# Block sums of four w_out pairs: made in DRAM by accumulating transfers in place of a page and VectorE additions

## The chip, the cores and the metric

The kernel runs on one core of a Trainium2 chip. The metric is device time in microseconds of one launch; before the change its median over three runs is 1105.4 us (1105.19 to 1105.71). The names used are those of the profile: PE is TensorE's matmuls, PEld its weight loads, DVE is VectorE, ACT is ScalarE, POOL is GpSimd, and SP is SyncE, whose in-order queue issues nearly all loads.

## The reference

One encoder block on x (256 tokens by 2048 channels), float32 throughout:

```python
hn = rmsnorm(h, mix_norm_pre)
z, xbc, dt_raw, u = split(hn @ w_in)
y_ssd = ssd_mixer(z, xbc, dt_raw, ...)   # bidirectional Mamba-2 scan, 16 heads
y_pool = pool_mixer(u, pool_w, pool_scale)
mix = concatenate([y_ssd, y_pool]) @ w_out          # w_out 2048 x 2048
h = h + rmsnorm(mix, mix_norm_post)
ff = conv_glu(rmsnorm(h, ffn_norm_pre), ...)         # 2048 -> 2 x 5632 -> 2048
h = h + rmsnorm(ff, ffn_norm_post)
gate = sigmoid(rmsnorm(h, ple_norm_pre) @ w_ple_gate)
h = h + rmsnorm(gate * (p @ w_ple), ple_norm_post)
```

The change lies in how part of `w_out` is made ready for the product `mix`.

## The kernel before

Float32 products are made of three TensorE products each: an operand is split into a high part (rounded to fp32r by an ACT copy, L157) and a low part (a DVE subtraction, L158). Weights arrive from DRAM as 1 MB tiles of 128 partitions by 2048, each a pair of k-blocks for 1024 output columns. `load` (L120) issues each on SP; the tile sits in one of three "raw" buffers, is split into one of five "w" buffers, and is multiplied. A raw buffer is free again when DVE has made the last low part from it, and until then SP waits with the next load, and with everything queued behind it.

The stages in order of time are: dt and pooling input (`dtu`, to about 49 us), the three slabs of `xbc` (`xb2`, `xb0`, `xb1`, 52 to 141 us, four 1 MB loads each), `z` (eight loads, 141 to 196 us) with the last scan products (`yo`, `yd`) between, the output projection (`wo`, 196 to 284 us), the gated feed-forward, its down projection `dn`, and the gate `gt`. Small jobs of the scan and the pooling are put into a list `work`; `aside()` runs one entry of it after every load's products, so that their PE, ACT and DVE instructions lie between those of the slabs. A scheduler sets the final order on each engine from the order of the code and its own model of times; a table of costs is not part of the program.

Some pairs of `w_out`, `w_down` and `w_gate` are multiplied by a scheme with seven block products for eight (`seven_products`), which needs, of the four 512-column blocks v0 to v3 of a weight tile, the sums that `add_blocks` makes (L275): v1+v0, v0+v3, v3+(v1+v0) and v2+v3+v1+v0. For four pairs of `w_out`, named (0, 0), (0, 2), (1, 0) and (1, 2) by output half and k-block, these sums are made early, while `xbc` and `z` run:

- `early_fetch` takes a page (one of 13 shared 1 MB buffers) and loads the pair into it (tile `wob`).
- `early_add` makes the sums in place with four DVE additions of 128 x 512, and GpSimd stores the page to a DRAM tile `wos` (L265).
- At 208.6 to 244.0 us `seven_products` loads `wos` back as `wo00t`, `wo02t`, `wo10t` and `wo12t`, and splits and multiplies it (`wo00c`, `wo00d` and so on).

What the steps below touch besides: `rz` and `yn0m` (the norm of y after the scan, small POOL operations at L804 and L410), `dec` (L608, POOL), `seg`, `E`, `cb`, `cv` (scan and convolution jobs on ACT, DVE and PE), `pw`, `mx`, `cath`, `catl` (pooling) and `sp` (the softplus of dt, a chain of small DVE operations at L577 to L589).

Of the kernel before, what the change touches and what calls it, by code (L numbers as in the profile page):

```python
# [11 lines left out]
F32 = mybir.dt.float32  # L12
F32R = mybir.dt.float32r
AF = mybir.ActivationFunctionType
ALU = mybir.AluOpType
ORDERED = (mybir.EngineType.Activation, mybir.EngineType.DVE, mybir.EngineType.SP)

P = 128
# [35 lines left out]
def build(nc, a, out):  # L54
    x = a["x"][0]

    w_dtu, w_xbc, w_z, w_out, w_up = a["w_dtu"], a["w_xbc"], a["w_z"], a["w_out_"], a["w_up"]
# [3 lines left out]
    with tile.TileContext(nc) as tc, \  # L61
# [9 lines left out]
        def ins(r):  # L71
            return getattr(r, "ins", r)

        def page(name, dtype=F32):
            return gp.tile([P, 2048], dtype, tag="pg", bufs=13, name=name)

        def mid(name, dtype=F32):
            return gp.tile([P, 1024], dtype, tag="mid", bufs=3, name=name)
# [4 lines left out]
        def main(name):  # L83
            return [pm.tile([P, 512], F32, tag="main", name=f"{name}_{i}") for i in range(2)]
# [30 lines left out]
        last, sums_ = {}, {}  # L115

        def load(dst, src, ahead=False):

            with tc.issue_after(last["dma"]) if last and not ahead else nullcontext():
                return ins(nc.sync.dma_start(dst, src))  # L120
# [79 lines left out]
        work = []  # L200
# [31 lines left out]
        def block_sums(name, w, c0, k, held):  # L232


            pg = []

            def fetch():
                r = page(f"{name}b{c0}_{k}")
                pg.append(r)
                load(r, w[c0 // 1024, k // 2])  # L240

            def add():
                add_blocks(pg[0])
                if held:
                    sums_[name, c0, k] = pg[0], True

            def store():
                if not held:
                    t = dp.tile([P, 2048], F32, tag=f"{name}s{c0}_{k}", bufs=1, name=f"{name}s{c0}_{k}")
                    nc.gpsimd.dma_start(t, pg[0])  # L250
                    sums_[name, c0, k] = t, False

            return fetch, add, store

        early_raw = {}

        def early_fetch(c, k):
            early_raw[c, k] = page(f"wob{c}_{k}")
            load(early_raw[c, k], w_out[c, k // 2])

        def early_add(c, k):
            r = early_raw.pop((c, k))
            add_blocks(r)
            t = dp.tile([P, 2048], F32, tag=f"wos{c}_{k}", bufs=1, name=f"wos{c}_{k}")
            nc.gpsimd.dma_start(t, r)  # L265
            sums_["wo", c * 1024, k] = t, False

        APART = ("dn",)

        def add_blocks(r, t=None):  # L270

            v = r.rearrange("p (b c) -> p b c", b=4)
            s = v if t is None else t.rearrange("p (b c) -> p b c", b=4)
            for i, a, b in ((1, v, 0), (0, v, 3), (3, s, 1), (2, s, 3)):
                nc.vector.tensor_add(s[:, i], v[:, i], a[:, b])  # L275
# [95 lines left out]
        def feature_major(name, w, get, acc):  # L371

            for u in range(4):
                r = raw(f"{name}r{u}", w[u])
                for j in range(2):
                    wh, wl = split(f"{name}{u}_{j}", r[:, j * 1024:(j + 1) * 1024], 1024)
                    for kk in range(2):
                        k = 4 * u + 2 * j + kk
                        xh, xl = get(k)
                        for f in range(4):  # L380
                            s = slice(kk * 512 + f * P, kk * 512 + (f + 1) * P)
                            for q, (ww, xx) in enumerate(((wh, xh), (wh, xl), (wl, xh))):
                                mm(acc[f // 2][:, f % 2 * L:(f % 2 + 1) * L], ww[:, s], xx,
                                   k == 0 and q == 0 and f % 2 == 0, k == NK - 1 and q == 2)
                aside()
# [19 lines left out]
        def rms(name, parts, scale, n=1):  # L405

            base = EPS
            for i, q in enumerate(parts):
                m = tiny(f"{name}m{i}", n)
                nc.gpsimd.tensor_scalar(m, q, scale, base, op0=ALU.mult, op1=ALU.add)  # L410
                base = m
            r = tiny(f"{name}r", n)
            nc.gpsimd.tensor_tensor(r, m, mhalf[:, :n], op=ALU.pow)
            return r
# [36 lines left out]
        def times_rows(name, acc, rb):  # L451
            o = mid(name)
            for i in range(2):
                nc.vector.tensor_tensor(o[:, i * 512:(i + 1) * 512].rearrange("p (f t) -> p f t", f=2),
                                        acc[i].rearrange("p (f t) -> p f t", f=2),
                                        rb.unsqueeze(1).to_broadcast([P, 2, L]), op=ALU.mult)
            return o

        def conv(name, acc, taps, wcol, wstep, bcol):

            cv = mid(name)
            half = taps // 2
            for f in range(4):
                o, i = cv[:, f * L:(f + 1) * L], acc[:, f * L:(f + 1) * L]
                nc.scalar.activation(o, i, AF.Identity, bias=vec(bcol + f), scale=vec(wcol + half * wstep + f))
                for j in range(taps):
                    d = j - half
                    if d == 0:
                        continue
                    lo, hi = max(0, -d), L - max(0, d)  # L470
                    nc.vector.scalar_tensor_tensor(o[:, lo:hi], i[:, lo + d:hi + d], vec(wcol + j * wstep + f),
                                                   o[:, lo:hi], op0=ALU.mult, op1=ALU.add)
            return cv
# [15 lines left out]
        for u in range(0, NK, 2):  # L489
            r = [wp.tile([P, 2048], F32, tag="raw", bufs=3, name=f"dtur{u}") if u else r0, page(f"dtur{u + 1}")]  # L490
            for j in range(2):
                k = u + j
# [17 lines left out]
            for j in range(2):  # L510
                k = u + j
# [184 lines left out]
        def xbc(slab):  # L696
            acc = main(f"xbc{slab}")
            feature_major(f"xb{slab}", w_xbc[slab], hn, acc)
            sc = times_rows(f"xr{slab}", acc, rxb)
            cv = conv(f"cv{slab}", sc, 5, V_SCW + 4 * slab, 12, V_SCB + 4 * slab)  # L700
            th = mid(f"th{slab}")
            nc.scalar.activation(th, cv, AF.Tanh, scale=0.5)

            nc.vector.scalar_tensor_tensor(cv, th, 1.0, cv, op0=ALU.add, op1=ALU.mult)
            return cv
# [42 lines left out]
        def job(f, *args):  # L748
            return lambda: f(*args)
# [5 lines left out]
            [job(pool_mix, 2), job(pool_mix, 3), job(decays), job(seg_sums)],  # L755
            [],
        ])
        work[0].append(job(early_fetch, 0, 0))
        work[2].append(job(early_add, 0, 0))
        work[1].append(job(early_fetch, 0, 2))  # L760
        work[3].append(job(early_add, 0, 2))
        work[3].append(job(early_fetch, 1, 0))
        bc = xbc(2)
        work.extend([
            [job(seg, 0), job(seg, 1), job(pool_map, 0), job(pool_map, 1)],
# [1 line left out]
            [job(seg, 4), job(weigh, 0, 0), job(pool_map, 2)],  # L767
            [job(seg, 5), job(pool_map, 3)],
        ])
        work[0].append(job(early_add, 1, 0))  # L770
        xa = xbc(0)
        work.extend([
            [job(seg, 6)],
# [1 line left out]
            [job(xs_turn, xa, 0)],  # L775
            [],
        ])
        xb = xbc(1)
        y = page("y")

# [8 lines left out]
            [job(mix, 0, 1), job(mix, 1, 0)],  # L789
            [job(mix, 1, 1)],  # L790
        ])
        work[4].append(job(early_fetch, 1, 2))
        work[6].append(job(early_add, 1, 2))
        zacc = [main(f"z{t}") for t in range(2)]
        token_major("z", w_z, 0, list(range(NK)), hn, zacc)
        assert not work
# [5 lines left out]
        for t in range(2):  # L802
# [13 lines left out]
            r = rms(f"yn{t}", [ss], rz[t][:, 1:2], n=2)  # L816
# [157 lines left out]
        for i, w_ in enumerate(which[2:] + which[:2]):  # L974
            fetch, add, store = block_sums(*w_, i >= len(which) - 2)
            n = 45 * i // 10 + 4
# [110 lines left out]
        with in_order():  # L1087
            for _ in range(5):
                next_part()
            for n in range(NPIECES):  # L1090
                s, v, i = blocks[n // 4]
# [135 lines left out]
        for half in range(2):  # L1227
# [16 lines left out]
            for t in range(2):  # L1244
                for n, (o, c0) in enumerate(columns(acc[t])):
                    c1 = c0 + o.shape[-1]
                    c = slice(half * 1024 + c0, half * 1024 + c1)

                    th = mid(f"gth{half}{t}{n}")
                    v = th[:, :c1 - c0]  # L1250
# [103 lines left out]
```

## Time and profile before

| | us |
|---|---|
| median of three runs | 1105.4 |
| the profiled execution, its time | 1104.97 |
| its span, first to last instruction | 1103.2 |
| PE busy | 1096.7 (99%) |
| DVE busy | 977.2 (89%) |
| ACT busy | 729.1 (66%) |
| POOL busy | 84.9 (8%) |

The profiled execution took 1104.97 us, 1.8 us more than its span and 0.4 us less than the median. Busy times are sums over the span. Matmuls overlap each other in the pipeline, so that the busy share of PE does not show short delays between matmuls; their starts do. The granted TensorE clock was 0.999 of full speed over the span.

### The profile page before, as it was taken

The page shows a single profiled execution, that of the slowest core. Times are in us where ns is not written, and L with a number is a line of the kernel's source. Part 1 is how long each engine was busy: PE and PEld are TensorE (multiplying, and loading weights), DVE is VectorE, ACT ScalarE, POOL GpSimd, SP SyncE. Part 2 cuts the span into 40 slices and gives each one's busy share as a digit, 9 for nine tenths or more (in the row PEclk, how much of TensorE's full clock was granted, in tenths as well). Part 3 has the DMA queues.
Part 4 walks back from the last instruction along what each step waited for, and adds up shares of the span by engine and source line. Part 5 has one row for each costly group of instructions (what it writes and reads, how often), then busy time and mean ns, then how long its engine had stood idle before and what let it go on. Part 6 is the DMA issues. An engine that isn't in the chain of part 4 may idle for free.

```text
span 1103.2 us, 16052 instructions
## 1 busy us (share of the span) xinstructions
PE 1096.7 (99%) x5961; PEld 948.8 (86%) x5961; DVE 977.2 (89%) x1373; ACT 729.1 (66%) x1068; POOL 84.9 (8%) x145
## 2 busy tenths in 40 slices
PE   9999999999999999999999999999999999999998
PEld 9999988888888888888888888888888888888886
DVE  6589998898868998889889988898999999999997
ACT  6858763566776565655656646657688878786773
POOL 0200000100100000000000000000000000051001
PEclk9999999999999999999999999999999999999999
DMA  9895259556489999989999998999999989996872
GB/s 363 359 339 195 101 183 367 209 195 244 158 367 388 408 397 364 403 344 367 383 366 383 364 391 345 404 362 420 367 410 375 378 335 389 419 379 224 317 276 77
DMA packets 57247, 361.71 MB, mean 328 GB/s; under 512 B 6352, under 2 KB 7504, under 8 KB 21200
## 3 DMA queue, kind: packets, MB, share of 16 engines
q1 hardware_dynamic: 45648, 298.71, 69.0%
q0 software_dynamic: 11088, 61.35, 14.5%
q8 instruction: 47, 0.77, 0.3%
q10 hardware_dynamic: 432, 0.62, 0.2%
q14 instruction: 32, 0.26, 0.1%
HBM read 306.65 MB, written 54.00 MB: 327 GB/s over the span
## 4 chain that ended last, share of the span: by engine, by line
PE 97%; ACT 1%; DVE 1%; issue 0%; POOL 0%; POOLq 0%; DVEq 0%
PE ga L90 22%; PE va L90 22%; PE dna L90 11%; PE woa L90 7%; PE xbc L90 5%; PE gt L90 5%; PE dns L90 4%; PE dtu L90 4%; PE z L90 4%; PE dn0s L90 2%; PE dn1s L90 2%; PE ple L90 1%; PE gts L90 1%; PE wos L90 1%; PE yd L90 1%; PE pw L90 1%
## 5 line engine op out<-in xcount | busy, mean ns | idle before, releaser
L90 PE MATMUL ga<-wox,ug_0w 128*128 128x512 f32 x704 | 130.8, 337 | 0.0
L90 PE MATMUL ga<-wox,ug_1w 128*128 128x512 f32 x704 | 130.2, 337 | 0.0
L90 PE MATMUL va<-wox,uv_0w 128*128 128x512 f32 x704 | 129.2, 337 | 0.0
L90 PE MATMUL va<-wox,uv_1w 128*128 128x512 f32 x704 | 129.2, 337 | 0.0
L90 PEld LDWEIGHTS ga<-wox,ug_0w 128*128 128x128 f32 x704 | 107.7, 188 | 14.6 <-ACT pl L919 0.2
L90 PEld LDWEIGHTS ga<-wox,ug_1w 128*128 128x128 f32 x704 | 107.5, 188 | 14.5 <-DVE wox L195 0.2
L90 PEld LDWEIGHTS va<-wox,uv_1w 128*128 128x128 f32 x704 | 107.5, 188 | 14.5
L90 PEld LDWEIGHTS va<-wox,uv_0w 128*128 128x128 f32 x704 | 107.5, 188 | 14.5
L275 DVE TENSOR_TENSOR dnb<-dnb 128x512 f32<-128x512 f32 x128 | 88.3, 690 | 3.0
L250 POOL DMA_DIRECT2D dns<-dnb x30 | 16.1, 536 | 319.4 <-DVE dnb L275 279.1
L90 PE MATMUL xbc<-hnh,xb_0w 128*128 128x256 f32 x192 | 37.9, 284 | 0.3 <-ACT u L571 0.3
L90 PE MATMUL xbc<-hnh,xb_1w 128*128 128x256 f32 x192 | 37.1, 283 | 0.0
L846 ACT CAST he<-he 128x512 fp32r<-128x512 f32 x13 | 8.1, 621 | 42.6 <-DVE he L845 42.6
L988 ACT CAST hs<-hid 128x384 fp32r<-128x384 f32 (+1 forms) x44 | 23.4, 537 | 13.7 <-PE dna L90 13.5
L90 PEld LDWEIGHTS xbc<-hnh,xb_0w 128*128 128x128 f32 x192 | 30.8, 189 | 0.9 <-ACT u L571 0.4
L90 PEld LDWEIGHTS xbc<-hnh,xb_1w 128*128 128x128 f32 x192 | 30.7, 189 | 0.1
L1068 ACT ACTIVATE fc<-gr,vt 128x256 f32<-128x256 f32 x44 | 26.1, 593 | 6.9 <-DVE gr L1061 6.9
L90 PE MATMUL dna<-dn_0w,hs 128*128 128x512 f32 x108 | 28.6, 394 | 0.0
L90 PE MATMUL dna<-dn_1w,hs 128*128 128x512 f32 x108 | 28.3, 392 | 0.0
L1139 POOL DMA_DIRECT2D hd<-hsum x24 | 12.9, 539 | 193.1 <-PE dn0s L90 70.4
L989 DVE TENSOR_TENSOR hs<-hid,hs 128x384 fp32r<-128x384 f32 (+1 forms) x44 | 25.4, 581 | 2.6 <-ACT hs L988 2.6
L90 PE MATMUL xbc<-hnl,xb_1w 128*128 128x256 f32 x96 | 27.3, 284 | 0.0
(1781 smaller groups left out, 2871.4 us busy)
## 6 DMA issues: line engine op xcount, KB each, us to landing
dnb<-w_down SPq DMA_DIRECT2D x32, 1024.0 KB, 10.0
dns<-dnb POOLq DMA_DIRECT2D x30, 1024.0 KB, 6.5
hd<-hsum POOLq DMA_DIRECT2D x24, 512.0 KB, 8.2
zr<-w_z SPq DMA_DIRECT2D x8, 1024.0 KB, 5.0
dtur<-w_dtu SPq DMA_DIRECT2D x14, 528.0 KB, 8.5
hsum<-he POOLq DMA_DIRECT2D x13, 512.0 KB, 7.7
wo0r<-w_out_ SPq DMA_DIRECT2D x6, 1024.0 KB, 6.2
gtb<-w_gate SPq DMA_DIRECT2D x6, 1024.0 KB, 9.6
```

What stands on the lines that cost most here:

```text
L90: last["pe"] = ins(nc.tensor.matmul(o, lhsT, rhs, start=start, stop=stop, skip_group_check=True))
L250: nc.gpsimd.dma_start(t, pg[0])
L275: nc.vector.tensor_add(s[:, i], v[:, i], a[:, b])
L846: nc.scalar.copy(o[:, :512], s[:, :512])
L988: nc.scalar.copy(t[:, :c1], hid_part(k)[:, :c1])
L989: nc.vector.tensor_sub(t[:, 512:512 + c1], hid_part(k)[:, :c1], t[:, :c1].bitcast(F32))
L1068: nc.scalar.activation(c[:, f], v[:, f], AF.Identity, bias=vec(V_FCB + 4 * s + 2 * i + f), scale=vec(w + NF))
L1139: nc.gpsimd.dma_start(o.bitcast(F32), kept[k])
```

## The change

`early_fetch` and `early_add` go, and with them four pages, the sixteen DVE additions (L275, `wob`) and four stores from GpSimd. In their place stands `sums_in_dram`, with three jobs for each pair:

- `copy`: SP copies the 1 MB of `w_out` to the DRAM tile `wos`, DRAM to DRAM, with no on-chip buffer.
- `pairs_`: two accumulating transfers issued by GpSimd. One adds block 3 of `w_out` to blocks 0 and 2 of `wos`, the other block 0 to blocks 1 and 3. Each has 256 rows of 2 KB.
- `rest`: two more, of 128 rows of 2 KB. One adds block 1 of `wos` to its block 2, the other block 1 of `w_out` to block 3.

The results are the same four sums. The loads back (`wo00t` and the rest), the splits and the products stay. The jobs stand one load apart in `work`, and the last pair's copy moves from the fifth entry of the `z` list to its second.

```diff
-        early_raw = {}
-
-        def early_fetch(c, k):
-            early_raw[c, k] = page(f"wob{c}_{k}")
-            load(early_raw[c, k], w_out[c, k // 2])
-
-        def early_add(c, k):
-            r = early_raw.pop((c, k))
-            add_blocks(r)
+        def sums_in_dram(c, k):
+
             t = dp.tile([P, 2048], F32, tag=f"wos{c}_{k}", bufs=1, name=f"wos{c}_{k}")
-            nc.gpsimd.dma_start(t, r)
-            sums_["wo", c * 1024, k] = t, False
+            src = w_out[c, k // 2]
+            o, v = (u.rearrange("p (b c) -> p b c", b=4) for u in (t, src))
+
+            def add(dst, from_):
+                nc.gpsimd.dma_start(dst, from_, accum_op=ALU.add)
+
+            def copy():
+                load(t, src)
+
+            def pairs_():
+                add(o[:, 0::2], v[:, 3:4].to_broadcast([P, 2, 512]))
+                add(o[:, 1::2], v[:, 0:1].to_broadcast([P, 2, 512]))
+
+            def rest():
+                add(o[:, 2], o[:, 1])
+                add(o[:, 3], v[:, 1])
+                sums_["wo", c * 1024, k] = t, False
+
+            return copy, pairs_, rest
...
-        work[0].append(job(early_fetch, 0, 0))
-        work[2].append(job(early_add, 0, 0))
-        work[1].append(job(early_fetch, 0, 2))
-        work[3].append(job(early_add, 0, 2))
-        work[3].append(job(early_fetch, 1, 0))
+        for n, j in enumerate(sums_in_dram(0, 0)):
+            work[1 + n].append(j)
...
-        work[0].append(job(early_add, 1, 0))
+        for n, j in enumerate(sums_in_dram(0, 2)):
+            work[1 + n].append(j)
...
+        for n, j in enumerate(sums_in_dram(1, 0)):
+            work[1 + n].append(j)
...
-        work[4].append(job(early_fetch, 1, 2))
-        work[6].append(job(early_add, 1, 2))
+        for n, j in enumerate(sums_in_dram(1, 2)):
+            work[1 + n].append(j)
```

On SP, before the change, where the loads of `xbc` (`xb2r`, `xb0r`, `xb1r`) are issued; `wob` is a page of the old way:

```order
L120 DMA poolw<-pool_w_ 128x2048
L120 DMA xb2r_765<-w_xbc 128x2048
L120 DMA wob_0_691<-w_out_ 128x2048
L120 DMA xb2r_866<-w_xbc 128x2048
L120 DMA xb0r_959<-w_xbc 128x2048
L120 DMA xb0r_1075<-w_xbc 128x2048
L120 DMA xb0r_1163<-w_xbc 128x2048
L120 DMA wob_2_763<-w_out_ 128x2048
L120 DMA xb0r_1264<-w_xbc 128x2048
L120 DMA wob_0_928<-w_out_ 128x2048
```

The same place after it:

```order
L120 DMA poolw<-pool_w_ 128x2048
L120 DMA wos_0_633<-w_out_ 16x16384
L120 DMA xb2r_763<-w_xbc 128x2048
L120 DMA xb2r_860<-w_xbc 128x2048
L120 DMA xb0r_948<-w_xbc 128x2048
L120 DMA xb0r_1058<-w_xbc 128x2048
L120 DMA wos_2_945<-w_out_ 16x16384
L120 DMA xb0r_1147<-w_xbc 128x2048
L120 DMA xb0r_1250<-w_xbc 128x2048
```

The first copy stands one place ahead of the first page load, before the third `xb2r` load, and the second copy one place ahead of the second. The third and fourth stand further on, behind the second `xb1r` load and behind the second load of `z`; the fourth page load stood behind all eight loads of `z`.

On POOL, before, from the norm constants `rz` to the norm of y:

```order
L805 TENSOR_SCALAR rz_2055<-rx0r 128x1
L265 DMA wos_0_864<-wob_0_691 128x2048
L608 TENSOR_TENSOR dec<-dec,dt 128x16 x2
L265 DMA wos_2_926<-wob_2_763 128x2048
L265 DMA wos_0_1073<-wob_0_928 128x2048
L265 DMA wos_2_2005<-wob_2_1890 128x2048
L410 TENSOR_SCALAR yn0m_2069<-ss_2060,rz_2055 128x2
```

The same after, as far as the second pair, and the fourth (the third reads as the others do), with the semaphores that each waits for (DMAHW: a transfer of SP, DMASW: one of POOL):

```order
L262 DMA wos_0_633<-w_out_ 256x1x512 [waits DMAHW2_49]
L262 DMA wos_0_633<-w_out_ 256x1x512
L262 DMA wos_0_633<-wos_0_633 128x512 [waits DMASW1_49,DMASW0_49]
L262 DMA wos_0_633<-w_out_ 128x512
L262 DMA wos_2_945<-w_out_ 256x1x512 [waits DMAHW7_49]
L262 DMA wos_2_945<-w_out_ 256x1x512
L618 TENSOR_TENSOR dec<-dec,dt 128x16 [waits DVE_49,Activation_49]
...
L262 DMA wos_2_1666<-w_out_ 256x1x512 [waits DMAHW1_49]
L262 DMA wos_2_1666<-w_out_ 256x1x512
L262 DMA wos_2_1666<-wos_2_1666 128x512 [waits DMASW6_49,DMASW5_49,DMASW4_49]
L262 DMA wos_2_1666<-w_out_ 128x512 [waits DMASW7_49]
L420 TENSOR_SCALAR yn0m_2061<-ss_2052,rz_2047 128x2 [waits Activation_49,Pool_49]
```

Four transfers stand where one stood, POOL waits for the copy before the first and for the first two before the third, and `dec` and `yn0m` stand behind such waits.

On DVE, before, from the end of the second `xb2r` load's split, with the softplus `sp` and the first pair's additions:

```order
L583 TENSOR_TENSOR sp_600<-sp_599 128x64
L275 TENSOR_TENSOR wob_0_691<-wob_0_691 128x512
L584 TENSOR_SCALAR sp_601<-sp_600 128x64
L275 TENSOR_TENSOR wob_0_691<-wob_0_691 128x512
L586 SCALAR_TENSOR_TENSOR sp_601<-sp_601,sp_600 128x64
L275 TENSOR_TENSOR wob_0_691<-wob_0_691 128x512
L586 SCALAR_TENSOR_TENSOR sp_601<-sp_601,sp_600 128x64
L275 TENSOR_TENSOR wob_0_691<-wob_0_691 128x512
L586 SCALAR_TENSOR_TENSOR sp_601<-sp_601,sp_600 128x64
L158 TENSOR_TENSOR xb_0w<-xb2r_866,xb_0w 128x1024
```

The same place after:

```order
L593 TENSOR_TENSOR sp_600<-sp_599 128x64
L594 TENSOR_SCALAR sp_601<-sp_600 128x64
L596 SCALAR_TENSOR_TENSOR sp_601<-sp_601,sp_600 128x64 x6
L597 SCALAR_TENSOR_TENSOR sp_601<-sp_601,sp_599 128x64
L158 TENSOR_TENSOR xb_0w<-xb2r_763,xb_0w 128x1024
L598 TENSOR_SCALAR sp_601<-sp_601 128x64
L158 TENSOR_TENSOR xb_1w<-xb2r_763,xb_1w 128x1024
```

The additions are gone and the softplus now runs ahead of the third load's split, which it stood behind.

## The prediction

> **What bounds the kernel now.** I read the busy times first, then the chain of work that ended last, then the chain piece by piece in the stages that the change touches, then the stretches of time with their DMA share, and last the waits of SP and the rows of single loads.
>
> ```profile
> span 1103.2 us, 16052 instructions
> PE 1096.7 (99%) x5961; PEld 948.8 (86%) x5961; DVE 977.2 (89%) x1373; ACT 729.1 (66%) x1068; POOL 84.9 (8%) x145
> PE 97%; ACT 1%; DVE 1%; issue 0%; POOL 0%; POOLq 0%; DVEq 0%
> ```
>
> TensorE is busy for 99% of the span and is 97% of the chain. Work taken off another engine is worth only what PE loses while it waits for that engine, in the stages where the work lay: `xbc` and `z`, 52 to 196 us. Busy time hides short delays between matmuls, so I count PE's work there by the chain's own pieces, which give a price for each kind:
>
> ```profile
> 52.24 11.71 PE xbc L90 x96
> 71.52 1.85 PE mx L90 x16
> 74.55 1.02 PE dps L90 x8
> 76.02 1.02 PE cps L90 x8
> 90.91 0.23 PE seg L90
> 101.73 0.86 PE cb L90 x4
> 118.38 1.43 PE pw L90 x12
> 134.07 0.88 PE xt L693 x8
> 134.95 5.72 PE xbc L90 x48
> 140.67 22.09 PE z L90 x96
> 182.87 0.86 PE yo L90 x2
> 183.73 1.73 PE yd L90 x16
> 196.31 11.10 PE woa L90 x48
> ```
>
> From the first `xbc` matmul (52.24) to the first of `z` (140.67) pass 88.43 us. By the code that stretch holds 12 loads of 48 `xbc` matmuls (12 x 5.72 = 68.6 us), two groups of 16 `mx` (3.7), `dps` and `cps` (2.0), 48 `pw` (4 x 1.43 = 5.7), two groups of four `cb` (1.7), 16 `seg` (16 x 0.23 = 3.7) and one group of `xt` (0.9): 86.3 us. PE lost at most 2.1 us there, 0.19% of the kernel, and not all of that to waits. From 140.67 to 196.31, 55.64 us, lie two times 96 `z` matmuls (44.2), four groups of `yd` (6.9), four of `yo` (3.4) and one of `xt` (0.9), 55.4 us: it lost 0.2. So no relief of DVE, SP or the pages in these stages can bring more than 2.1 + 0.2 = 2.3 us.
>
> **The change, part by part.** *The additions.* DVE loses the sixteen additions:
>
> ```profile
> L275 DVE TENSOR_TENSOR wob<-wob x16: 678/684/694, 60.3 to 177.4; 128x512 f32<-128x512 f32 x16
> 52.20:140.70 88.50, 88.26 (x705) 85.98 (x706) 82.62 (x153) 61.47 (x104) 3.15 (x5) 1.00 0.57 208
> 78.59 1.05 ACT xb_1w L157
> 88.68 0.48 ACT E L636
> ```
>
> That is 16 x 0.684 = 10.9 us of DVE work, 8.2 us of it in the `xbc` stage, where DVE works 82.6 of 88.5 us (the third of the busy times in the row, after PE and PEld). Yet PE already works there without a break worth 2.1 us, and where the chain does leave PE, from 78.59 to 89.16 us, it runs through ACT, which loses no instruction. So the cover that hides the additions is PE itself; it stays. I take 0.3 us of gain out of the possible 0 to 2.3, nearer to the low end because the row of the chain names ACT and not DVE.
>
> *The new order.* On DVE the softplus comes earlier, and on PE, ACT and DVE the `seg`, `pw`, `cb` and `catl` jobs between 88 and 130 us stand a few rows from where they stood. Nothing in the trace prices a new order. Below, the gain is already in the 2.3 us. Above, I bound it by one split of half a load that comes late as a whole, since a weight tile is the largest thing that PE takes at a time:
>
> ```profile
> 53.70 1.22 DVE L158 TENSOR_TENSOR xb_1w<-xb2r,xb_1w 128x1024 fp32r<-128x1024 f32 x1
> 60.88 1.05 ACT L157 CAST xb_0w<-xb2r 128x1024 fp32r<-128x1024 f32 x1 [3.49 <-DMA xb2r<-w_xbc]
> 73.37 1.19 PE xbc L90 x10
> ```
>
> 1.05 + 1.22 = 2.3 us. I take nothing: the splits run far ahead of PE. The half load that ACT waited 3.49 us for and split at 60.88 is the fourth of its slab, and PE starts on it at 73.37: 12.5 us of lead.
>
> *SP.* Four loads leave the queue and four copies enter it, so its issue time stays. The copies need no page, so SP no longer stands still for one. What it does stand still for is the raw buffers:
>
> ```profile
> SPq L120 <- DVE xb_1w L158: 65.0, 9, 16.3
> 37.64 0.39 SPq L120 DMA_DIRECT2D xb2r<-w_xbc  x1
> 116.72 46.50 SPq L120 DMA_DIRECT2D zr<-w_z  x8
> 40.00:50.00 10.00, 10.00 (x64) 10.00 (x63) 0.36 (x2) 9.86 (x14) 1.44 (x5) 1.00 1.01 420
> 90.00:100.00 10.00, 9.98 (x82) 9.73 (x81) 10.00 (x16) 6.45 (x11) 0.00 (x0) 1.00 0.14 43
> 110.00:120.00 10.00, 10.00 (x80) 9.63 (x79) 9.59 (x16) 8.81 (x15) 0.00 (x0) 1.00 0.21 76
> ```
>
> The first copy is issued where the third `xb2r` load was, at about 38 us, when the DMA engines are full (share 1.01, 420 GB/s, the last two numbers of the row), ahead of the third `xb2r` load. It delays that load by its own 1 MB, 1.05 MB / 420 GB/s = 2.5 us, or twice that if a copy inside DRAM costs a read and a write. PE gets to that load at 52.24 + 2 x 5.72 + 1.85 = 65.5 us, over 25 us after its issue, so this is hidden. The second copy passes two `xb0r` loads, the third two `xb1r` loads, the fourth six `z` loads, each by the same 2.5 to 5 us against a lead of 12.5: nothing.
>
> *The accumulating transfers.* For each pair they write 2 x 256 + 2 x 128 = 768 rows of 2 KB, 1.57 MB, where one 1.05 MB store was; the page load becomes the copy. No row shows an accumulating transfer. The nearest are these:
>
> ```profile
> poolw<-pool_w_ SPq DMA_DIRECT2D x1, 1024.0 KB, 11.7
> wos<-wob POOLq DMA_DIRECT2D x4, 1024.0 KB, 4.7
> out<-vg SPq DMA_DIRECT2D x6, 256.0 KB, 2.8
> ```
>
> At the 26 GB/s per engine of the full stretch, a 2 KB row takes 0.08 us and the 48 rows that each of 16 engines gets take 3.7 us a pair; below that it cannot go. The high end is a row that waits out a whole transfer, 2.8 us by the shortest landing shown: 48 x 2.8 = 134 us a pair. I take the low end doubled for the two operands, 7.5 us a pair, because the nearest row, the store by the same queue to the same tile, landed in 4.7 us, only 2.2 us over its bytes. One sentence of the Trainium skill bears on this, in "Collectives: The Full Stack", section "The bandwidth ceiling": a reducing transfer runs at half the rate of a copy because it has two sources to read, while the addition is free. No run so far shows it; by it the estimate would be 7.5 us a pair, by the plain row 3.7, and neither comes near the points below.
>
> With 2.2 us of landing a step, a pair then takes 12 us or so for its copy (11.7 at worst, as `poolw` in the full stretch), and 7.2 and 4.7 us for its two steps. The first pair is ready at about 38 + 12 + 12 = 62 us, the last, whose copy goes out behind the second `z` load (the eight spread over 46.50 us from 116.72) at about 123 us, at about 147. What waits for them is late:
>
> ```profile
> 63.47 0.77 POOL L265 DMA_DIRECT2D wos<-wob  x1 [21.32 <-DVE sp L586]
> 194.98 0.58 POOL L410 TENSOR_SCALAR yn0m<-ss,rz 128x2 f32<-128x2 f32 x1 [16.09 <-ACT zt L815]
> 208.64 0.37 SPq L120 DMA_DIRECT2D wo00t<-wos  x1
> 216.85 1.05 ACT L157 CAST wo00dw<-wo00t 128x1024 fp32r<-128x1024 f32 x1 [1.03 <-DMA wo00t<-wos]
> ```
>
> Behind POOL's new waits stand `dec`, used by the `yo` products (182.87 us in a row above), and `yn0m` at 194.98; on SP `wo00t` waits from 208.64. All have some 50 us or more. POOL's own cost, 16 issues for 4 at the 0.77 us of the first row, perhaps double for 256 rows, is some 18 us of an engine that is 8% busy.
>
> **Sum.** Additions -0.3, new order 0, SP 0, transfers 0: the profiled execution's 1104.97 us would become 1104.7. The median stands 0.4 us above that execution, so I predict 1105.4 - 0.3 = 1105.1 us.
>
> **Rivals.** *Slow accumulation crowds out the weights (slower).* A load has 64 KB for each engine, eight packets of 8 KB, 0.31 us each at 26 GB/s. If the engines take turns by packet and an accumulating row costs p, a load beside it takes 8 x (0.31 + p). The 48 rows of a pair last as long as six loads, and PE uses up six loads in 6 x 5.72 = 34.3 us. PE stalls once 48 x (0.31 + p) is more than 34.3 + 12.5 of lead, that is from p = 0.67 us, eight times the plain price. At 0.8 us it is 53.3 - 46.8 = 6.5 us a pair, 26 us for four: 1131 us. For it: no row prices these transfers, and round trips of 2.8 us exist. Against it: stores by the same queue run at the full rate. 8%.
>
> *The new order makes PE wait.* A job of ACT or DVE that now stands ahead of a split that PE needs costs up to the 2.3 us above: 1107.7. For it: ACT has hardly a gap between 80 and 90 us. Against: 12.5 us of lead and DVE with 11 us less to do. 5%.
>
> *The relief is worth the whole loss.* If everything that PE lost was DVE's lateness, it is 1105.4 - 2.3 = 1103.1 us. Against it stand the chain's ACT pieces. 4%.
>
> *The change does nothing that shows.* The additions were hidden and so are the transfers; this is the forecast, 1103.2 to 1107.6, 83%.
>
> **How the numbers follow.** About 0.2%, 2.2 us, is what a measurement of this kernel can tell from no change. The forecast's case lies within it. Faster is the third rival, 4%; slower the first two, 8 + 5 = 13%. The range takes the bounds of the two terms that are not known, 2.3 us of gain below and 2.3 us of a late split above, 1103.1 to 1107.7; it leaves out the first rival and what lies beyond these bounds, under two in ten.
>
> **What the profile after would show.** Right: no `wob` rows; DVE busy 11 us less; PE busy and chain as before; the first `z` matmul within 2 us of 140.67; the four pairs' last transfers landed before 160 us; no wait of ACT for `wo00t` longer than some 1 us. Wrong: a landing of the two 256-row transfers above 21 us (32 rows for each engine at 0.67 us), ACT waiting for `xb0r`, `xb1r` or `zr`, POOL holding `yn0m` past 195 us, or the first `woa` later than 196.31 by more than 2 us. A gain of over 2.3 us would mean that I counted PE's losses wrongly.

## The result and the profile after

Eight runs of each kernel on one chip: 1108.34 us after (1107.25 to 1110.02) against 1105.46 us before (1105.12 to 1105.71). The ratio is 1.0028, 95% interval 1.0017 to 1.0038. The kernel is slower by 2.9 us, above the 1107.7 us at which the predicted range ended. The profiled execution took 1109.73 us and is one of the two longest; why it lies 1.4 us above the median is told with the clock below.

The page after, its first lines and its chain:

```profile
span 1108.0 us, 16048 instructions
PE 1099.5 (99%) x5961; PEld 950.7 (86%) x5961; DVE 968.5 (87%) x1357; ACT 727.9 (66%) x1068; POOL 97.2 (9%) x157
PE 95%; DVE 1%; ACT 1%; DMA 1%; issue 0%; POOL 0%; POOLq 0%; DVEq 0%; ACTq 0%
```

DVE is relieved and PE is busy for longer. The chain, 97% PE before, now holds 1% of DMA time. Here is that DMA piece in the chain from 55 to 78 us, with the first rows of `z` and of the output projection:

```profile
55.02 13.36 DMA xb2r<-w_xbc
...
68.47 1.06 ACT xb_0w L157
...
73.05 0.61 DVE mixl L665
...
73.71 2.84 PE mx L90 x16
76.55 2.05 PE xbc L90 x10
...
144.65 22.09 PE z L90 x96
...
200.29 11.10 PE woa L90 x48
```

Before, `mx` stood at 71.52 us and took 1.85 us, and the ten `xbc` matmuls after it 1.19 us. First `z` was at 140.67 and is now 144.65 (4.0 us later); first `woa` was at 196.31 and is now 200.29 (4.0). So the whole loss of these stages arises between 71 and 79 us, beside the first pair's transfers. The other three pairs add nothing up to 200 us. Some 0.7 us more of the span arise in the gate `gt`, after 1020 us: its matmuls end in the chain at 1085.1 us before and at 1089.8 after, 4.7 us later; why is not shown.

What PE and ACT wait for (waited for, us in total, times, longest):

```profile
PE mx L90 <- DVE mixl L665: 2.1, 1, 2.1
```

```profile
ACT xb_0w L157 <- DMA xb2r<-w_xbc: 11.0, 1, 11.0
ACT z_0w L157 <- DMA zr<-w_z: 10.6, 3, 5.9
```

PE had no wait at `mx` before, and ACT waited 3.5 us for that load instead of 11.0. The rows of ACT show how the one becomes the other:

```profile
56.40 1.07 ACT L157 CAST xb_1w<-xb2r 128x1024 fp32r<-128x1024 f32 x1
68.47 1.05 ACT L157 CAST xb_0w<-xb2r 128x1024 fp32r<-128x1024 f32 x1 [11.00 <-DMA xb2r<-w_xbc]
69.43 1.04 ACT L157 CAST xb_1w<-xb2r 128x1024 fp32r<-128x1024 f32 x1
70.75 1.05 ACT L157 CAST xb_0w<-xb0r 128x1024 fp32r<-128x1024 f32 x1 [0.28 <-DMA xb0r<-w_xbc]
71.70 1.07 ACT L664 CAST mixh<-mx 128x512 fp32r<-128x512 f32 x2
```

and before:

```profile
64.98 0.58 ACT L654 CAST mixh<-mx 128x512 fp32r<-128x512 f32 x1
```

ACT takes its instructions in order. The split of the fourth `xb2r` load stands ahead of the `mixh` casts, small pooling work that needs no load. These casts (with `mixl`, DVE's low part, behind them) empty the `mx` accumulators, which PE needs for its next `mx` products before it comes to the late load itself. They came at 71.70 instead of 64.98.

Why the load was late: the DMA view of 50 to 85 us, after and then before. `DMA` and `GB/s` are 40 slices of 0.875 us; the other rows give KB of each transfer and us from issue to landing.

```profile
DMA  9513699689899999999999975988996899999999
GB/s 403 234 75 21 84 94 98 51 73 98 105 187 243 325 279 283 346 323 372 424 421 552 777 318 211 365 190 136 169 154 133 293 398 370 370 332 290 257 241 190
...
wos<-w_out_ POOLq DMA_DIRECT2D x4, 512.0 KB, 14.1
xb2r<-w_xbc SPq DMA_DIRECT2D x1, 1024.0 KB, 13.4
```

```profile
GB/s 412 262 84 19 0 0 75 103 412 431 403 431 403 300 431 412 281 365 449 318 290 337 374 421 421 421 393 346 346 262 309 431 375 47 150 403 365 309 346 346
...
xb2r<-w_xbc SPq DMA_DIRECT2D x1, 1024.0 KB, 5.8
```

In both kernels the load is issued at about 55 us. Before, the engines stood empty and it ran at 412 GB/s from 57 us. After, they are occupied for six to more than nine tenths of the time from 53.5 us by the two accumulating transfers that GpSimd issued at 51.2, and move only 51 to 105 GB/s up to 59.6 us. Counted in the trace's DMA records, no packet of the load starts before 60.6 us; before the change its first started at 55.9. By 60.5 us 347 of the 512 accumulating rows of 2 KB had started; from 60.6 to 67.4 us records of the remaining rows and of loads start side by side. POOL's rows give the length of the steps, since it waits for the first two transfers before it issues the third (the first and third pair's):

```profile
51.17 2.38 POOL L262 DMA_DIRECT2D wos<-w_out_  x2 [9.02 <-DMA wos<-w_out_]
68.71 0.84 POOL L262 DMA_DIRECT2D wos<-wos  x1 [15.16 <-DMA wos<-w_out_]
...
108.72 2.13 POOL L262 DMA_DIRECT2D wos<-w_out_  x2 [12.96 <-DMA wos<-w_out_]
122.70 0.83 POOL L262 DMA_DIRECT2D wos<-wos  x1 [11.86 <-issue]
...
198.97 0.58 POOL L420 TENSOR_SCALAR yn0m<-ss,rz 128x2 f32<-128x2 f32 x1 [38.56 <-ACT zt L825]
```

The first step took 68.71 - 51.17 = 17.5 us, the third pair's 14.0 us, and the other two pairs' 17.7 and 18.7; the forecast had 7.2. So all four pairs were slow, and PE waited beside the first alone.

After the wait the clock falls. In 1 us stretches (PE, PEld, DVE, ACT and POOL busy, granted clock, DMA share, GB/s):

```profile
73.00:74.00 1.00, 0.29 (x2) 0.29 (x3) 1.00 (x3) 1.00 (x2) 0.00 (x0) 1.00 0.81 129
74.00:75.00 1.00, 1.00 (x11) 1.00 (x11) 1.00 (x2) 0.72 (x2) 0.00 (x0) 0.97 0.90 127
75.00:76.00 1.00, 1.00 (x7) 1.00 (x6) 1.00 (x2) 0.52 (x1) 0.00 (x0) 0.50 1.16 174
...
77.00:78.00 1.00, 1.00 (x6) 1.00 (x6) 0.81 (x2) 0.17 (x1) 1.00 (x2) 0.50 0.77 281
78.00:79.00 1.00, 1.00 (x10) 1.00 (x9) 0.00 (x0) 0.00 (x0) 0.50 (x1) 0.82 1.04 367
```

PE works at half the clock for some 3.4 us: 0.03 + 3 x 0.50 + 0.18 = 1.7 us lost. With the 2.1 us of waiting that is 3.8 of the 4.0 us. The lower clock does not come in every run: in six of the eight the mean granted clock is 0.999 or 1.000 at 1107.25 to 1108.89 us, in the profiled one and one more 0.997 and 0.998 at 1109.73 and 1110.02 us. By this the median's loss of 2.9 us is mostly the wait itself; as only the profiled execution has a trace, that is inferred and not shown.

### The profile page after: what moved, and what is told of

It reads as the page before. It is cut to its first block, busy times and chain, and to the rows that moved or that the text cites. A ratio compares the mean times of both kernels' runs of the same rounds, so it can differ in the third digit from the quotient of the medians.

```text
span 1108.0 us, 16048 instructions
## 1 busy us (share of the span) xinstructions
PE 1099.5 (99%) x5961; PEld 950.7 (86%) x5961; DVE 968.5 (87%) x1357; ACT 727.9 (66%) x1068; POOL 97.2 (9%) x157
## 4 chain that ended last, share of the span: by engine, by line
PE 95%; DVE 1%; ACT 1%; DMA 1%; issue 0%; POOL 0%; POOLq 0%; DVEq 0%; ACTq 0%
PE ga L90 22%; PE va L90 22%; PE dna L90 11%; PE woa L90 6%; PE gt L90 5%; PE dns L90 4%; PE dtu L90 4%; PE z L90 4%; PE xbc L90 4%; PE dn0s L90 2%; PE dn1s L90 2%; DMA xb2r<-w_xbc 1%; PE ple L90 1%; PE gts L90 1%; PE wos L90 1%; PE yd L90 1%
## 5 line engine op out<-in xcount | busy, mean ns | idle before, releaser
L90 PE MATMUL xbc<-hnl,xb_0w 128*128 128x256 f32 x96 | 27.7, 288 | 0.0
```

The source lines that it names most:

```text
L90: last["pe"] = ins(nc.tensor.matmul(o, lhsT, rhs, start=start, stop=stop, skip_group_check=True))
```

## The experiments

My theory after reading this profile (the queue theory): the transfers of the first pair occupy the DMA engines while a load is due that ACT waits for, and the price is set by what stands behind that wait. The rivals: the price lies in the accumulating rows wherever they stand; it lies in the new order of instructions or in the copies; or each pair pays its share.

**The first pair the old way.** Pair (0, 0) goes back to a page, four additions and a store; the other three stay.

```diff
...
-        for n, j in enumerate(sums_in_dram(0, 0)):
-            work[1 + n].append(j)
+        work[0].append(job(early_fetch, 0, 0))
+        work[2].append(job(early_add, 0, 0))
```

> Only the first pair (0, 0) goes back to a page, four VectorE additions and a store; the other three pairs stay in DRAM. Queue theory: the loss is one stall, begun by the first pair's accumulating transfers, which delay the fourth xb2r load, on which ScalarE stands with the mixh casts behind it. Then the median is 1105.0 to 1105.7, ScalarE waits for that load 3 to 4 us instead of 11.0, and TensorE has no wait at mx. Rival (each pair costs its share, by its transfers or by the new order of jobs): three quarters of the 2.9 us stay, 1107.2 to 1108.

1105.3 us against 1105.03, ratio 1.0007 (0.9997 to 1.0017). PE has no wait at `mx`. ACT's wait is the old one:

```profile
ACT xb_0w L157 <- DMA xb2r<-w_xbc: 3.5, 1, 3.5
```

Three pairs of four cost nothing that can be measured here (the interval would still admit 1.9 us), and with the first pair the wait and its loss are gone.

**Only the first pair the new way.** The reverse: (0, 0) in DRAM, and the other three with pages.

```diff
-        for n, j in enumerate(sums_in_dram(0, 2)):
-            work[1 + n].append(j)
+        work[1].append(job(early_fetch, 0, 2))
+        work[3].append(job(early_add, 0, 2))
...
```

> Only the first pair is made in DRAM; the other three go back to pages and VectorE additions, at their old places. Queue theory: the whole loss stays, 1107.3 to 1110, with ScalarE waiting some 11 us for the fourth xb2r load. Rival (each pair its share): a quarter of the loss, 1106.0 to 1106.4.

1113.24 us, ratio 1.0082 (1.0061 to 1.0103), more than either expected. The profile has the same wait at `mx`, and a second one:

```profile
PE seg L90 <- ACT E L659: 2.4, 1, 2.4
PE mx L90 <- DVE mixl L678: 2.2, 1, 2.2
```

```profile
DVE wob L298 <- DMA wob<-w_out_: 4.5, 1, 4.5
```

The page load of a second pair now also arrives late: SP, held up longer at the `xb0r` loads, issues it at 71.8 us instead of 66.1, and it lands after 10.6 us, beside the first pair's second step. DVE, in order, stands 4.5 us at the additions, with the `seg` jobs behind them, and PE waits. The granted clock is 0.83 in each of the two 10 us stretches with a wait, 1.7 us each, so that waits and clock together are 4.6 + 3.4 = 8.0 us. The same mechanism strikes twice, and the old way pays for a neighbour of the new.

**Plain rows.** The same sixteen transfers without the addition (each overwrites its blocks; the sums are not made).

```diff
-                nc.gpsimd.dma_start(dst, from_, accum_op=ALU.add)
+                nc.gpsimd.dma_start(dst, from_)
```

> The sixteen GpSimd transfers keep their rows, sources, places and waits but overwrite instead of adding, so the sums are not made. If the price is in the accumulation (two operands to read, a write that needs both), the rows of 2 KB take 0.08 us as other 2 KB rows do instead of 0.18, the first pair's first step ends in under 8 us instead of 17, the fourth xb2r load lands by 63 us and the time is 1105 to 1106. If any row of 2 KB from DRAM to DRAM on GpSimd's queue does it, it stays at 1107 to 1110.

1107.08 us, ratio 1.0019 (1.0011 to 1.0028): about two thirds of the loss stay. Of the two cases of the expectation the second came, at its low end: the addition is not the price, or not the greater part of it.

```profile
ACT xb_0w L157 <- DMA xb2r<-w_xbc: 8.4, 1, 8.4
```

```profile
PE dps L90 <- DVE mixl L665: 1.2, 1, 1.2
```

By POOL's issues the first step takes 12.0 us instead of 17.5. So 512 rows of 2 KB from DRAM to DRAM are slow with or without the sum: 12.0 us is 0.37 us for each of an engine's 32 rows, where a stream at the full 26 GB/s has 0.08. The control is not exact: the DMA records of this run move the rows in pieces of 4 KB, two rows to a piece, where those of the changed kernel have one record a row.

**Copies only.** The accumulating transfers are left out; the copies, the new order and the absence of pages stay (the sums are not made).

```diff
             def pairs_():
-                add(o[:, 0::2], v[:, 3:4].to_broadcast([P, 2, 512]))
-                add(o[:, 1::2], v[:, 0:1].to_broadcast([P, 2, 512]))
+                pass
...
-                add(o[:, 2], o[:, 1])
-                add(o[:, 3], v[:, 1])
```

> The four copies from DRAM to DRAM stay, at their places on SyncE's queue; all sixteen accumulating transfers are left out, so the sums are not made. Queue theory, as it now stands (the accumulating transfers, and not the copy, keep the fourth xb2r load back): the load lands within 7 us of its issue, ScalarE waits 3 to 4 us for it, and the time is 1104.8 to 1105.6. Rival (the copy ahead of the third load, or the new order of jobs, makes part of the loss): 1106 to 1107.5.

1105.37 us against 1104.75, ratio 1.0002 (0.9991 to 1.0013); ACT's wait for `xb2r` is 3.5 us. The copies on SP, the removed additions and the new order together are worth nothing that can be measured (the interval would admit 1.4 us).

**The first step twice.** The two transfers of the first pair's first step are issued a second time behind themselves (block sums of that pair then hold an addend too many).

```diff
+                if (c, k) == (0, 0):
+                    add(o[:, 0::2], v[:, 3:4].to_broadcast([P, 2, 512]))
+                    add(o[:, 1::2], v[:, 0:1].to_broadcast([P, 2, 512]))
```

> As the kernel after, but the first pair's first step is issued a second time into the same tile (its sums are then wrong), so that one more MB of accumulating rows lies beside the loads from about 62 to 75 us. Queue theory: the first loads of xb0 are now late too, by some 6 to 8 us, ScalarE stands on them ahead of the second mixh casts, and the loss grows from 2.9 us to between 6 and 12: 1111 to 1117. Rival (a cost per transfer, not a stall): 0.2 us more for two transfers, under 1109.5.

1111.35 us, ratio 1.0052 (1.0031 to 1.0073); by the two ratios 0.0024 x 1105 = 2.7 us more than the changed kernel. The median is inside the range given, at its low end.

```profile
PE mx L90 <- DVE mixl L668: 3.2, 1, 3.2
```

The wait grows by 1.1 us only, and the half clock lasts from 74 to 81 us instead of 75 to 78. The fourth `xb2r` load is no later than in the changed kernel (ACT's wait for it is 10.6 us), for by POOL's rows the repeats, each waiting for the transfer before it, were issued at 62.7 and 69.2 us, when that load was under way. The `xb0r` load after it is the one that lands late, and the casts wait for its split too; but ACT splits it at 72.44 us, 1.7 us later than in the changed kernel, and not the 6 to 8 us that were expected. The interval is wide and the clock takes much of the difference, so that this run supports the queue theory and does not measure it.

**The casts ahead of the late split.** If ACT's order turns a late load into a wait of PE, the remedy is to put the `mixh` casts ahead of that split.

```diff
-                    wh, wl = split(f"{name}{u}_{j}", r[:, j * 1024:(j + 1) * 1024], 1024)
+                    with tc.issue_after(last["mix1"]) if (name, u) == ("xb2", 3) else nullcontext():
+                        wh, wl = split(f"{name}{u}_{j}", r[:, j * 1024:(j + 1) * 1024], 1024)
...
-            nc.scalar.copy(mixh[:, c], ps)
+            last[f"mix{g}"] = ins(nc.scalar.copy(mixh[:, c], ps))
```

> All four pairs in DRAM; the two splits of the fourth xb2r load are ordered behind the first two mixh casts on ScalarE, so that these do not stand behind a load. Queue theory: the load is as late as before (lands near 68 us), but TensorE gets its mx banks in time and its weights at about 71, before it needs them at 73.4; the time is 1105.0 to 1106.0 and no TensorE wait at mx is left. Rival (the weights themselves come too late for TensorE): the stall moves to the fourth load's products and the time stays at 1107 to 1110.

1108.44 us, ratio 1.0033 (1.0021 to 1.0045): missed. The wait at `mx` is gone, and there is one at the next products, since the second pair of casts now stands behind a late `xb0r` load (and the granted clock is 0.90 and 0.93 in the two 10 us stretches from 70 us on, 1.7 us more):

```profile
PE dps L90 <- DVE mixl L666: 1.2, 1, 1.2
```

**Both pairs of casts ahead.** The same with the second pair also put ahead of the `xb0r` split that held it.

```diff
+                    behind = {("xb2", 3): "mix1", ("xb0", 1): "mix3"}.get((name, u))
+                    with tc.issue_after(last[behind]) if behind else nullcontext():
```

> As the kernel after, with both pairs of mixh casts ordered ahead of the load that they stood behind (the fourth xb2r load, the second xb0r load). With the first pair alone moved, the stall went from the first pair of casts to the second. Queue theory: no TensorE wait at mx or dps is left though the loads land as late as before (67 to 73 us), and the time is 1105.0 to 1106.0. Rival (the late loads themselves are the limit, wherever the casts stand): the wait moves on to the weights of xb2 or xb0 and the time stays at 1107 to 1109.

1108.13 us, ratio 1.0025 (1.0013 to 1.0036): missed again. A short wait at `dps` stays, and the longer ones have moved on by 20 to 30 us, to where the second pair's transfers run:

```profile
PE cb L90 <- DVE catl L195: 1.5, 1, 1.5
...
PE xbc L90 <- DVE xb_1w L158: 1.3, 1, 1.3
PE dps L90 <- DVE mixl L667: 0.6, 1, 0.6
```

```profile
93.76 8.41 DMA xb1r<-w_xbc
...
102.25 1.05 ACT xb_0w L157
103.30 0.39 ACT cath L194
```

An `xb1r` load lands 8.4 us after its issue, and the `cath` cast that PE is due to use stands right behind its split. 1.5 + 1.3 + 0.6 = 3.4 us of waits; the first `z` is at 144.15 us, 3.5 later than before.

**Its control: that order, copies only.** The order of the last kernel, with the accumulating transfers left out as above.

> The order of e6 (both pairs of mixh casts ahead of the two load splits that they stood behind) with the accumulating transfers left out and the copies kept; the sums are not made. It is the control for e6. If the stalls of e6 at 93 to 104 us come from the transfers delaying an xb1r load: 1105 to 1106, like the copies alone in the old order (1105.4), no wait of PE over 0.5 us there. If the new order itself is what makes a split late: 1107 to 1108.5, like e6 (1108.1), with the waits of PE for catl or xb_1w still there.

1105.83 us against 1105.09, ratio 1.0004 (0.9996 to 1.0013). The waits at `cb` and `dps` are gone and one remains, against the expectation that there would be none:

```profile
PE xbc L90 <- DVE xb_1w L158: 1.3, 1, 1.3
```

That one belongs to the order (a split on DVE that comes late), and it is nearly made good elsewhere: the first `z` is at 141.15, 0.5 us later than before. The other waits, 1.5 + 0.6 us, are the transfers'.

**Every pair one slab later.** (0, 0) beside `xb0`, (0, 2) beside `xb1`, (1, 0) and (1, 2) from the second and fifth load of `z`.

```diff
-        for n, j in enumerate(sums_in_dram(0, 0)):
-            work[1 + n].append(j)
         bc = xbc(2)
...
-        for n, j in enumerate(sums_in_dram(0, 2)):
+        for n, j in enumerate(sums_in_dram(0, 0)):
             work[1 + n].append(j)
         xa = xbc(0)
...
         for n, j in enumerate(sums_in_dram(1, 2)):
-            work[1 + n].append(j)
+            work[4 + n].append(j)
```

> All four pairs are made in DRAM, each begun one slab later: (0, 0) in the xb0 slab, (0, 2) in xb1, (1, 0) and (1, 2) in z at its second and fifth load. Queue theory: the fourth xb2r load meets no accumulating transfer, the first begins at about 70 us, and the time is 1104.6 to 1105.6, as with the first pair on its page; the last pair is ready before 200 us, and nothing waits for it. Rival (wherever these transfers lie beside loads they cost some 0.7 us a pair): 1107 to 1108.5.

1106.76 us, ratio 1.0021 (1.0001 to 1.0041), in two groups: six runs of 1104.7 to 1105.7 us, five of 1110.4 to 1111.7 and one of 1107.8, the profiled one. The median lies between the ranges that the theory and its rival gave, so it decides for neither. The first wait is gone, as expected (no wait at `mx`). In the profiled run the transfers of two pairs delay the loads of `z` and the first of `wo0`. The chain there:

```profile
178.62 8.17 DMA wo0r<-w_out_
...
186.89 1.06 ACT wo_0w L157
...
189.81 0.61 DVE ym L749
...
190.46 2.00 PE yd L90 x16
```

`y` and `ym`, small jobs that the scan products need, stand on DVE behind the low part of a weight tile that came late. PE waits 1.9 us. Why five of the runs took 5 us or more longer and six took nothing more is not shown: only one run has a trace. Not all of it need be the change's, for three of the 31 runs of the kernel before that were taken beside these took 1111.2 to 1111.8 us too; those had a granted clock of 1.000, four of the five here one of 0.996 or 0.997.

**Three pairs one slab later, the fourth the old way.** So that no pair runs beside the last `xb2r` load, and only one beside `z`; the edit is against the kernel just told of.

```diff
...
-        for n, j in enumerate(sums_in_dram(1, 2)):
-            work[4 + n].append(j)
+        work[4].append(job(early_fetch, 1, 2))
+        work[6].append(job(early_add, 1, 2))
```

> Three pairs by the new way, each one slab later than in the changed kernel (beside xb0, xb1 and the beginning of z), and the pair (1, 2) the old way with page, additions and store. So no pair's transfers run beside the last xb2r load, and only one pair's beside z. If a pair's transfers cost only where a waiting load has a needed instruction behind it, and e7 lost its time to two pairs in z: 1104.8 to 1105.8, no wait of PE for mx or ym over 0.5 us. If every pair costs its share wherever it stands: about three quarters of the changed kernel's loss, 1107.3 to 1108.

1105.41 us against 1105.09, ratio 1.0004 (0.9993 to 1.0015). PE has no wait over 0.3 us in these stages, though the transfers are as slow, and the loads of `z` as late, as in the changed kernel:

```profile
68.43 2.40 POOL L275 DMA_DIRECT2D wos<-w_out_  x2 [26.26 <-DMA wos<-w_out_]
84.59 0.84 POOL L275 DMA_DIRECT2D wos<-wos  x1 [13.76 <-DMA wos<-w_out_]
```

```profile
ACT z_0w L157 <- DMA zr<-w_z: 10.6, 3, 6.1
```

The first pair's first step of 16.2 us delays no load that ACT waits for (between 66 and 115 us it waits for none), and the 10.6 us of waiting for `zr`, which the changed kernel has as well, cost nothing: no wait of PE follows from them, so that nothing that PE needs soon stood behind them. No kernel with pairs in DRAM was measurably faster than the kernel before.

## Why the prediction was wrong

*What held.* No run gained more than the 2.3 us that PE's own losses allow, and taking work from DVE brought nothing that can be measured (copies only: 1.0002). DVE's busy time fell by 8.7 us, where 10.9 were forecast. The copies and SP's queue cost nothing that can be measured. `dec` and `yn0m` did not suffer from POOL's waits: `yn0m` came at 198.97 us, later by 4.0 like everything after 79 us.

*The lead of the loads: the step that failed.* I took the fourth `xb2r` load's lead from ACT's split at 60.88 to PE's use of that load at 73.37: 12.5 us. That left out the split itself, 1.05 + 1.22 us; but above all ACT is in order, and behind that split stood casts that PE needs earlier. From that split to the `mx` matmuls lie 73.71 - 68.47 = 5.24 us of work, and PE was due there at 71.52. The split could start at 71.52 - 5.24 = 66.3 us at the latest, so the lead was 66.3 - 60.9 = 5.4 us. It started 68.47 - 60.88 = 7.6 us late: 7.6 - 5.4 = 2.2 us, where the trace has a wait of 2.13. This is a bookkeeping of the profile after and no second proof, since the 5.24 us come from it; the proof lies in the experiments: without the first pair's transfers the delay and the wait are both gone, and with the casts ahead of the late split the wait at `mx` is gone though ACT gets to that split only at 67.7 us. That the lead was short could be seen ahead: the chain had `mx` at 71.52, and ACT's rows had `mixh` behind the split.

*The price of the accumulating rows: mis-sized.* I took 0.16 us a row and 7.2 us for a first step. The records have a median of 0.178 us of busy time for an accumulating row, against 0.084 for a row of 2 KB of a plain load (and 0.16 for the 4 KB pieces of the plain-rows run), so that the rule I cited from the Trainium skill, "Collectives: The Full Stack", section "The bandwidth ceiling" (two sources, half the rate), agrees with the trace for the row by itself. But the step took 17.5 us, 0.55 us for each of an engine's 32 rows. The first row started 2.0 us after the issue; up to 60.5 us the rows kept the engines busy for some nine tenths of the time at a mean of 0.31 us a row, well over the median; and the rest shared the engines with the loads. Why so many rows take longer than the median is not shown; even without the addition the step has 0.37 us a row. The last pair's rows ended at 166 us, where I had 147. My nearest row, the page's store at 4.7 us, was a transfer from an on-chip buffer in long rows, and so no neighbour. I had the high end of 2.8 us a row on the page and let the low end decide.

*The turns: wrong.* The rival "slow accumulation crowds out the weights" was the right mechanism with the wrong sum. It let a load take turns with the rows packet by packet, spread the loss over six loads and set its threshold at 0.67 us a row; by it 0.55 us would have done no harm. In the trace the load takes no turns at first: no packet of it starts for 5.6 us after its issue, and only then do its packets run beside the rows that are left. The landing of 17.5 us stayed under the 21 us that I had named as the sign, and the loss came all the same. And the rival charged every pair, 26 us for four, where one pair paid.

*The rival on the new order.* Its 2.3 us were the right size for a thing that did not happen by the order alone; the control shows one wait of 1.3 us that the order makes, nearly made good.

## What to carry to other kernels

The slack of a load is not the time until its own data are used: take the engine that waits for it, list what is queued behind the wait, and measure to the earliest of these that the bounding engine needs. A transfer that replaces compute is priced by how long it keeps the DMA engines from the loads that follow, and many short rows from DRAM to DRAM hold them far longer than their bytes say. Reordering behind one late load moved the wait to the next twice; moving three pairs to where nothing needed stood behind a waiting load, with the fourth on its page, removed it.

## What the runs showed of the hardware that was not expected

*A load behind queued rows starts late.* The Trainium skill, "DMA: Bandwidth & Descriptors", section "Queues, rings and completion order", says that an engine goes round its queues and changes over only when it has drained a whole packet, typically some 9 to 17 descriptors (the single pieces that a transfer is made of) and at most 64. Here the load's first packet started 5.6 us after its issue, when some 22 accumulating rows an engine had started (347 on 16 engines); before the change it started 1.0 us after the issue. A change-over after such long packets would fit this, and so would rows that simply go first: the records name no engine, so the runs do not decide.

*A short gap of PE can cost about twice its length.* 2.1 us without a matmul were followed by 3.4 us at a granted clock of 0.50, 1.7 us more. The same happened after a gap of 1.2 us (plain rows: 0.91 in 70 to 80 us; the casts ahead: 0.90), yet not after 1.9 us in the profiled run of "every pair one slab later" (1.00). Where it came, the half clock lasted 3.41 us each time, or twice that ("the first step twice", 6.83 us). The Trainium skill, "TensorE: Matmul & The Clock Gate", section "HAM oscillation — how this bites in real kernels", warns of gaps over about 3.4 us. The stretch at half clock is of that length here, but gaps well under it sufficed, in some runs and not in others; what decides is not shown.
